# Layer 0's scale columns formed by TensorE products, its start-up sums spread over the steps, and the value projection 512 columns wide

## The chip, the cores and the metric

One core of one Trainium2 chip runs the whole program. The metric is device time in microseconds (us) of one execution, lower is better. TensorE's engine (PE) runs at one of two clock levels, 1.2 and 2.4 GHz; the profile gives the granted share of the higher one.

## The reference

Four layers over 1024 latent tokens of width 1024, with 256 context tokens beside them. Layer 0 is a pooling mixer, layer 1 a neighbourhood attention, layer 2 a short convolution, layer 3 pooling again. Each layer scales and shifts the normed input by columns that come from a conditioning vector. What the change touches is this, cut:

```python
def _modulation(cond, w, b):
    m = jax.nn.silu(cond) @ w + b
    return jnp.split(m, 3, axis=-1)          # shift, scale, gate

hx = _rmsnorm(x, norm_g[i]) * (1.0 + scale[:, None]) + shift[:, None]
hc = _rmsnorm(ctx, norm_g[i]) * (1.0 + cscale) + cshift   # from c_ctx
u, g = jnp.split(h @ w_in, 2, axis=-1)       # layer 0 (pool mixer)
q, k, v, g = jnp.split(h @ w_in, 4, axis=-1) # layer 1 (attention)
```

There are two conditioning vectors, `c` for the latent tokens (called x in the kernel) and `c_ctx` for the context (called c). For each layer, 1024 shift, 1024 scale and 1024 gate values are needed for x, and in layers 0 and 1 also for c.

## The kernel before

Features lie on the 128 partitions, so a 1024-wide activation is eight tiles, numbered k. Every fp32 matrix product is done in three passes (`mm3`, L115 to L117): operands are split into a high part (on ScalarE, `split`, L79) and a low part (L80, on VectorE or GpSimd), and high-high, high-low and low-high are added in PSUM.

The conditioning columns come 128 at a time. `ada_tile` (L166) takes a 128 by 1024 tile of the layer's modulation weights, loaded with a 512 KB transfer, multiplies it on VectorE with the broadcast silu row of one conditioning vector and sums along the row: one VectorE instruction and an accumulator read for one column of 128 values, so two for x and c.

`start` is the beginning of layer 0. Its order on VectorE, ScalarE, GpSimd and SP is the order of the code (`manual_schedule`); PE's is the order of the code everywhere. Its first part is the loop over k in which five output tiles (`FIRST`: u6, u7, g6, g7, g4) are multiplied over the first 512 latent tokens as the eight input tiles come in: for each k a weight tile is split, the scale column for x is summed (L166) and turned into a gain (`gain`, L174), then `high` (L698, ScalarE) and `low` (L702, VectorE) scale the input into its two parts, and 15 matmuls of 512 columns follow. Five of the sums for the context's scale ride in steps 2 to 6 (`EARLY`), the other three in the second part. The squares for the norm are formed on ScalarE and added on GpSimd (L734, L736). The second part multiplies the same five tiles over the other 512 tokens, and beside it come the eight shift tiles (`fetch_shift`, `ada`, `ada_sum`): for x always on VectorE; for c on VectorE for three of the eight (`DV`) and for the other five as a product on GpSimd (L793), a sum on ScalarE (L798) and an addition on GpSimd (L799). The third part multiplies the five tiles over the context (258 columns: 256 tokens and the two shift columns), which needs all the context's scale and shift columns (`gained_c`, L805/L806, and `shift_c`).

After `start` the remaining tiles of layer 0 follow, with the pooling sums (L455 to L466) and, as `background`, further conditioning tiles; the numbers in `RATES` say how many of these go with each weight load. There the tile scheduler sets the order on all engines but PE.

`na_first` is the beginning of layer 1. `v_block` forms the values for one block of 128 tokens and one range of output columns: here the activations are the stationary operand and the weights move. Before the change a block has 256 columns (a quarter of the width): 40 blocks of 24 matmuls, 40 evacuations to a tile `v` with three buffers (L970, L971) and 40 transfers out (L972). Between blocks hooks (`tick`) normalise the rest of layer 1's input, and `background(1)` runs one conditioning tile, from the sixth group of blocks on of layer 2.

PSUM has eight banks, taken in turn by everything that PE writes. The slots `a` (4 KB a partition) number 33. All transfers go through SP's queue, in order.

Of the kernel before, what the change touches and what calls it, by code (L numbers as in the profile page):

```python
# [24 lines left out]
P = 128  # L25
D = 1024
# [27 lines left out]
class Net:  # L54
# [102 lines left out]
    def ada_tile(self, l, conds, j, raw=None):  # L157
# [222 lines left out]
    def pool_in(self, li, h, chunks, start=None):  # L380
# [114 lines left out]
        RATES = (0,0,0,0,3,0,5,4,3,0,6,5,5,5,8,6) if 'c' in chunks else (3, 0, 6, 6) * 4  # L495
# [57 lines left out]
    def consts(self):  # L553
# [3 lines left out]
        rows = [self.slot([1, D]) for _ in range(2)]  # L557
# [3 lines left out]
        for f in range(2):  # L561
            nc.sync.dma_start(rows[f][:], i["conds"][f])
        nc.sync.dma_start(self.x0[0], i["xT"][0, :, 0:HALF])
# [3 lines left out]
        cond = [self.bank() for _ in range(4)]  # L567
        for f in range(4):
            nc.tensor.matmul(cond[f], self.ones[0:1, :], rows[f // 2][:, f % 2 * HALF:(f % 2 + 1) * HALF], start=True, stop=True)
        self.cond = cond[2:]  # L570
        self.sil["c"] = self.slot([P, D])
# [4 lines left out]
        self.shifts = self.pc.tile([P, 2, 3 * KT], F32, name="M0")  # L576
        for c in range(2):
            self.AB[0, "xc"[c]] = (self.pc.tile([P, KT], F32, name=f"A0{c}"), self.shifts[:, c, :])
# [71 lines left out]
    def start(self, h, put, shift, W):  # L650
# [7 lines left out]
        raws, shifts, wraw, parts = {}, {}, {}, {}  # L658
# [23 lines left out]

        fetch_w(0)
        nc.sync.dma_start(self.vec[:], i["vecs"])
        fetch(0)
        nc.sync.dma_start(x0[1], i["xT"][1, :, 0:HALF])
        fetch(1)
        fetch_w(1)
        self.load_pair(x0, i["xT"], 2, 0)
        fetch(2)  # L690
        fetch_w(2)
        row = self.sil["c"]
# [10 lines left out]

        def gain(k):
            self.ada_tile(0, ["x"], KT + k, raws[k])
            self.gain(0, "x", k, k + 1)

        split_weight(0)
        gain(0)
        high(0, x0, 0)  # L710
        low(0, x0, 0)
        for f in range(2):
            nc.scalar.activation(row[:, f * HALF:(f + 1) * HALF], self.cond[f], AF.Silu)
        gain(1)
        high(0, x0, 1)
        low(0, x0, 1)
        ps = {t: self.bank() for t in tiles}
# [20 lines left out]
        squares = {1: ((0, 0),), 2: ((0, 1),), 3: ((0, 2),), 4: ((0, 3),), 6: ((1, 0), (1, 1)), 7: ((1, 2), (1, 3))}  # L738
        EARLY = {2: (0,), 3: (1,), 4: (2,), 5: (3,), 6: (4,)}
        for k in range(KT):  # L740
            if k + 3 < KT:
                fetch(k + 3)
                if k + 3 < len(tiles):
                    fetch_w(k + 3)
                if k % 2:
                    self.load_pair(x0, i["xT"], k + 3, 0)
            if k == 4:
                nc.sync.dma_start(self.ident[:], i["ident"])
                for q in range(0, KT, 2):
                    self.load_pair(x1, i["xT"], q, HALF)  # L750
            if k == 5:
# [13 lines left out]
            if k >= 6:  # L765
                for q in range(4 * k - 24, 4 * k - 20):
                    high(1, x1, q)
                for q in range(4 * k - 24, 4):
                    low(1, x1, q)
            for ch, j in squares.get(k, ()):  # L770
                square(ch, (x0, x1)[ch], j)
            for n, t in enumerate(tiles):
                if (k, n) == (KT - 1, 2):
# [765 lines left out]
```

## Time and profile before

| what | value |
|---|---|
| median of 3 runs | 1920.62 us (1918.4 to 1920.69) |
| the profiled execution | 1921.01 us |
| its span, first to last instruction | 1919.2 us |
| PE busy | 1849.5 us, 96% of the span |
| VectorE (DVE) busy | 1090.0 us, 57% |
| ScalarE (ACT) busy | 725.2 us, 38% |
| GpSimd (POOL) busy | 568.6 us, 30% |
| mean granted PE clock | 0.986 |

Busy shares are means over stages that differ. The page's 40 slices (48 us each) show PE and DVE both at 7 to 9 tenths in the first six slices (0 to 288 us), and PE at 9 (90% or more) from then on but for the last slice. The times of single stages are read from the windows and rows below.

### The profile page before, as it was taken

The numbers are of one execution on the slowest core, as the hardware profiler recorded it, in microseconds if no ns is written. First come the engines' busy times: TensorE is split into PE (matmuls) and PEld (weight loads), VectorE is DVE, ScalarE is ACT, GpSimd is POOL, SyncE is SP. The second block draws the span as 40 slices with busy tenths as digits, with TensorE's granted clock in tenths as the row PEclk, the third lists the DMA queues.
The fourth block names the chain that finished last, engine by engine and source line by source line (L and its number), as shares of the span: only waits on it lengthen the run. The fifth ranks groups of instructions, "written<-read, shape, count | busy, mean of one in ns | idle before, by whom it ended". The sixth has DMA issues, their size and how long they took to land.

```text
span 1919.2 us, 27001 instructions
## 1 busy us (share of the span) xinstructions
PE 1849.5 (96%) x9808; PEld 1591.8 (83%) x9808; DVE 1090.0 (57%) x2251; ACT 725.2 (38%) x1401; POOL 568.6 (30%) x548
## 2 busy tenths in 40 slices
PE   7889899999999999999999999999999999999997
PEld 4677778889998889999998977888888887888887
DVE  7989977347441146766768678444232336433627
ACT  3332215344222146666657666121121225322422
POOL 4645412652210024444334542000000024433120
PEclk9899999999999999999999999999999999999999
DMA  6233352544673557676678656443111254011234
GB/s 256 77 105 105 114 175 79 184 139 145 224 251 116 165 154 210 196 205 189 192 210 231 201 176 202 132 132 99 44 45 55 70 183 159 12 49 41 77 119 155
DMA packets 126384, 272.10 MB, mean 142 GB/s; under 512 B 12810, under 2 KB 48394, under 8 KB 126252
## 3 DMA queue, kind: packets, MB, share of 16 engines
q1 hardware_dynamic: 126252, 270.39, 44.8%
q8 instruction: 77, 1.26, 0.3%
q14 instruction: 55, 0.45, 0.1%
HBM read 217.58 MB, written 52.76 MB: 141 GB/s over the span
## 4 chain that ended last, share of the span: by engine, by line
PE 76%; DVE 14%; issue 3%; DMA 3%; POOL 2%; ACT 1%; SPq 0%; DVEq 0%; POOLq 0%; ACTq 0%
PE mm L115 22%; PE mm L117 22%; PE mm L116 22%; DVE junk L166 4%; PE O L1257 4%; DMA raw<-in_ada 2%; PE T L1229 2%; PE TB L1229 2%; PE S L1172 1%; DVE S L455 1%; POOL S L455 1%; PE S L1173 1%; DVE a L80 1%; DVE wlo L80 1%; PE SC L1175 1%
## 5 line engine op out<-in xcount | busy, mean ns | idle before, releaser
L115 PE MATMUL mm<-a,whi 128*128 128x512 f32 (+2 forms) x2160 | 820.4, 380 | 23.7 <-DVE U L418 11.2
L116 PE MATMUL mm<-a,whi 128*128 128x512 f32 (+2 forms) x2149 | 804.5, 374 | 10.1 <-DVE a L80 8.0
L117 PE MATMUL mm<-a,wlo 128*128 128x512 f32 (+2 forms) x2160 | 806.6, 373 | 2.7 <-POOL wlo L80 2.6
L115 PEld LDWEIGHTS mm<-a,whi 128*128 128x128 f32 x2160 | 411.3, 190 | 96.7 <-DVE U L418 12.3
L116 PEld LDWEIGHTS mm<-a,whi 128*128 128x128 f32 x2149 | 409.6, 191 | 79.8 <-DVE a L80 9.4
L117 PEld LDWEIGHTS mm<-a,wlo 128*128 128x128 f32 x2160 | 410.7, 190 | 75.2 <-POOL wlo L80 4.1
L79 ACT ACTIVATE whi<-raw 128x1024 fp32r<-128x1024 f32 (+2 forms) x237 | 170.9, 739 | 352.3 <-PE mm L116 271.1
L80 POOL TENSOR_TENSOR wlo<-raw,whi 128x256 fp32r<-128x256 f32 (+2 forms) x150 | 191.3, 1289 | 365.8 <-ACT whi L79 338.7
L80 DVE TENSOR_TENSOR wlo<-raw,whi 128x1024 fp32r<-128x1024 f32 (+1 forms) x87 | 108.7, 1250 | 114.5 <-ACT whi L79 112.9
L166 DVE CUSTOM_DVE_ANT_0 junk<-raw,sil_x,vec 128x1024 bf16<-128x1024 f32 x86 | 118.6, 1379 | 92.9 <-DMA raw<-in_ada 92.3
L1208 POOL TENSOR_SCALAR lg<-lg,rsum 128x640 f32<-128x640 f32 (+1 forms) x128 | 99.2, 775 | 236.9 <-DVE rsum L1207 198.5
L115 PE MATMUL mm<-a,a 128*128 128x512 f32 (+2 forms) x280 | 98.1, 350 | 9.0 <-ACT a L698 7.1
L1199 ACT ACTIVATE lg<-lg,nmx 128x640 f32<-128x640 f32 (+1 forms) x128 | 102.6, 801 | 7.5 <-DVE rsum L1207 5.4
L224 POOL TENSOR_TENSOR a<-a,a 128x512 f32<-128x512 f32 x42 | 58.1, 1384 | 146.1 <-ACT a L223 139.9
L1187 DVE TENSOR_SCALAR_CACHE_REDUCE lg<-SC 128x256 f32<-128x256 f32 x128 | 54.2, 423 | 81.7 <-PE SC L1175 74.2
L116 PE MATMUL mm<-a,a 128*128 128x512 f32 (+2 forms) x275 | 96.2, 350 | 3.3 <-DVE a L702 2.8
L117 PE MATMUL mm<-a,a 128*128 128x512 f32 (+2 forms) x280 | 96.9, 346 | 0.5 <-DVE a L80 0.5
L1232 ACT ACTIVATE pthi<-TB 128x256 fp32r<-128x256 f32 (+1 forms) x128 | 52.6, 411 | 90.9 <-PE TB L1229 88.3
L1189 DVE CUSTOM_DVE_ANT_0 lg<-S,bias,mx 128x384 f32<-128x384 f32 (+1 forms) x128 | 74.8, 584 | 4.6
L1257 PE MATMUL O<-pthi,a 128*128 128x256 f32 (+2 forms) x288 | 76.6, 291 | 0.0
L1257 PE MATMUL O<-ptlo,a 128*128 128x256 f32 (+2 forms) x288 | 76.2, 293 | 0.0
L79 ACT ACTIVATE a<-a 128x512 fp32r<-128x512 f32 (+2 forms) x90 | 43.3, 536 | 79.3 <-POOL a L1420 72.7
(178 smaller groups left out, 2537.9 us busy)
## 6 DMA issues: line engine op xcount, KB each, us to landing
raw<-in_ada SPq DMA_DIRECT2D x86, 512.0 KB
raw<-in_pool_out SPq DMA_DIRECT2D x32, 512.0 KB
raw<-in_conv_in SPq DMA_DIRECT2D x32, 512.0 KB
raw<-in_pool_in SPq DMA_DIRECT2D x27, 512.0 KB
x<-a SPq DMA_DIRECT2D x48, 256.0 KB
raw<-in_na_in SPq DMA_DIRECT2D x24, 512.0 KB
a<-dk SPq DMA_DIRECT2D x48, 256.0 KB
dv<-v SPq DMA_DIRECT2D x40, 256.0 KB
```

Of the source, the lines that this page charges most:

```text
L79: self.nc.scalar.activation(hi, src, AF.Copy)
L80: (lo_engine or self.nc.vector).tensor_tensor(lo, src, hi.bitcast(F32), op=ALU.subtract)
L115: t.matmul(ps, wh, hh, start=(begin and k == ks[0]), stop=False)
L116: t.matmul(ps, wh, hl, start=False, stop=False)
L117: t.matmul(ps, wl, hh, start=False, stop=(end and k == ks[-1]))
L166: nc.vector.tensor_tensor_reduce(out=junk[:], in0=raw[:], in1=self.sil[c][:], scale=1.0, scalar=self.vec[:, b:b + 1], op0=ALU.mult, op1=AL ...
L224: (engine or nc.gpsimd).tensor_tensor(acc, acc, sq[k % 2], op=ALU.add)
L1189: nc.vector.tensor_tensor_reduce(out=lg[:, 0:L], in0=S[:, 0:L], in1=bias[:, off:off + L], scale=-1.0, scalar=mc[:], op0=ALU.add, op1=ALU.m ...
L1199: nc.scalar.activation(pr[:, :L + CTX], lg[:, :L + CTX], AF.Exp, bias=nm[:], scale=-1.0, accum_out=sm[:])
L1208: nc.gpsimd.tensor_scalar(pr[:, :L], pr[:, :L], rs[:], 1.0, op0=ALU.mult, op1=ALU.mult)
L1229: nc.tensor.transpose(t[:, s * P:(s + 1) * P], pr[:, o:o + P], self.ident[:])
L1257: nc.tensor.matmul(ops[:, q * P:(q + m) * P], v, part[:, p:p + m, :], start=not second and n == 0 and part is hi, stop=bool(second) and n ...
```

## The change

Three things are changed.

First, the scale columns of layer 0. A new input `ada0` holds the scale part of the layer's modulation weights laid out as matmul weights, and `condT` the two conditioning vectors as columns. `ada_product` multiplies one 128 by 1024 tile of it with the silu of both vectors: eight fp32 matmuls with two moving columns, which gives one 128-wide column for x and one for c at once in PSUM. `gain` then makes both gains in one DVE instruction from PSUM. The eight L166 sums for x and eight for c are gone, and the silu row for c now comes as a broadcast transfer and one activation in place of two matmuls.

Second, the order of `start`. The shift tiles 0 to 4 are summed for x and c on DVE in steps 0 to 4 of the first loop (`total`, `SUMS = 5`), tiles 5 to 7 in the second part; the detour over GpSimd and ScalarE is gone. The gain and high part of step k+2 are issued after the second tile of step k, its low part after the x sum. The high and low parts of the other 512 tokens are spread over steps 5 to 7, three at a time, and no longer fill the norm's chain. The weight tile u4 is loaded and split inside `start`, so two numbers of `RATES` change places.

Third, the value projection: blocks of 512 columns, so 20 blocks of 24 matmuls, 20 evacuations, 40 transfers out as before; eight weight tiles as before, five of them in `a` slots in place of three. `tick` runs twice in a block, `background` two or three times.

```diff
+    def ada_product(self, raw):
+        ps = self.bank()[:, 0:2]
+        for q in range(KT):
+            self.nc.tensor.matmul(ps, raw[:, q * P:(q + 1) * P], self.cols[:, 2 * q:2 * q + 2], start=q == 0, stop=q == KT - 1)
+        return ps
...
-        RATES = (0,0,0,0,3,0,5,4,3,0,6,5,5,5,8,6) if 'c' in chunks else (3, 0, 6, 6) * 4
+        RATES = (0,0,0,0,0,3,5,4,3,0,6,5,5,5,8,6) if 'c' in chunks else (3, 0, 6, 6) * 4
...
+        nc.sync.dma_start(rows[:], i["conds"][0])
+        nc.sync.dma_start(self.cols[:], i["condT"])
+        nc.scalar.activation(self.cols[:], self.cols[:], AF.Silu)
...
-            nc.sync.dma_start(raws[k][:], i["ada"][0, KT + k])
+            nc.sync.dma_start(raws[k][:], i["ada0"][k])
...
         def gain(k):
-            self.ada_tile(0, ["x"], KT + k, raws[k])
-            self.gain(0, "x", k, k + 1)
+            ps = self.ada_product(raws.pop(k))
+            nc.vector.tensor_scalar(self.gains[:, :, k], ps, up[:, k:k + 1], self.vec[:, V_NG + k:V_NG + k + 1],
+                                    op0=ALU.add, op1=ALU.mult)
+        def total(j, conds):
+            for c in conds:
+                self.ada_tile(0, [c], j, sums[j])
...
-            for q in EARLY.get(k, ()):
-                self.ada_tile(0, ["c"], KT + q, raws.pop(q))
+            if k >= SUMS:
+                for q in range(3 * (k - SUMS), min(3 * (k - SUMS) + 3, KT)):
+                    high(1, x1, q)
+                    low(1, x1, q)
+            for n, t in enumerate(tiles):
+                if n == 2 and k + 2 < KT:
+                    gain(k + 2)
+                    high(0, x0, k + 2)
+                if (k, n) == (KT - 1, 2):
+                    first = self.rstd_sums(([sq[0][:, 0]], HALF))
+                self.mm3(ps[t], self.wk(W[t]), lambda q: h[0][q], (k,), begin=k == 0, end=k == KT - 1)
+            if k < SUMS:
+                total(k, "x")
             if k + 2 < KT:
-                gain(k + 2)
-                high(0, x0, k + 2)
                 low(0, x0, k + 2)
+            if k < SUMS:
+                total(k, "c")
...
-            if k not in DV:
-                nc.gpsimd.tensor_tensor(raw[:], raw[:], row[:], op=ALU.mult)
...
-                nc.scalar.activation(raw[:], raw[:], AF.Copy, accum_out=Mc[:, k:k + 1])
...
             if n == 0:
-                step(0)
+                total(5, "xc")
+                W["u", 4] = self.weight(i["pool_in"][0, 4], own=True, lo_engine=nc.gpsimd)
+            if n == 1:
                 spread(0, dg)
...
-            ps = self.bank()[:, :256]
-            self.mm3(ps, hs, lambda k: tuple(Wv[k // 4][s][:, (k % 4) * 256:(k % 4 + 1) * 256] for s in range(2)), range(KT))
+            ps = self.bank()
+            for ks in (range(4), range(4, KT)):
+                self.mm3(ps[:], hs, lambda k: tuple(Wv[k // 2][s][:, k % 2 * HALF:(k % 2 + 1) * HALF] for s in range(2)), ks,
+                         begin=ks[0] == 0, end=ks[0] > 0)
+                self.tick()
...
-        blocks = [(0, (0, 1, 2, 3)), (1, (0, 1, 2, 3)), (0, (4, 5, 6, 7)), (1, (4, 5, 6, 7)), (0, (8, 9)), (1, (8, 9)),
-                  (2, range(NB + 2)), (3, range(NB + 2))]
+        blocks = [(0, (0, 1, 2, 3)), (0, (4, 5, 6, 7)), (0, (8, 9)), (1, range(NB + 2))]
...
-                self.background(1)
+                self.background(3 if n == 3 else 2)
```

How the change moves instructions is shown at three places.

On DVE before, from one step of the first loop to the next: `junk` rows are L166 sums (with `sil_x` for x, with `a_154`, the silu row of c, for c), `A_159` is the gain column and the L702 row is the low part.

```order
L166 ISA junk_284,M_158<-a_244,sil_x,vec 128x1024
L166 ISA M_158 128x1
L174 SCALAR_TENSOR_TENSOR A_159<-M_158,vec 128x1
L702 SCALAR_TENSOR_TENSOR a_287<-a_134,A_159,a_287 128x512
L166 ISA junk_315,M_158<-a_178,a_154,vec 128x1024
```

On DVE in the changed kernel, the same stretch: the gain (L724) reads `mm_333`, a product in PSUM, and the low part is L716.

```order
L724 TENSOR_SCALAR A_154<-mm_333,up_186,vec 128x2
L166 ISA junk_354,M_153<-a_276,sil_x,vec 128x1024
L166 ISA M_153 128x1
L716 SCALAR_TENSOR_TENSOR a_343<-a_134,A_154,a_343 128x512
L166 ISA junk_357,M_153<-a_276,a_180,vec 128x1024
```

The sum no longer stands ahead of the gain that comes from it; a sum of a shift tile stands between the gain and the low part, where ScalarE forms the high part.

On PE in the changed kernel, between the second and the third tile of a step (before, the fifteen matmuls of a step stood without a break): `mm_381` is the product of the scale tile of the step after next.

```order
L117 MATMUL mm_220<-a_298,wlo_279 128x512
L174 MATMUL mm_381<-cols,a_272 128x2 x8
L115 MATMUL mm_221<-a_298,whi_278 128x512
L116 MATMUL mm_221<-a_298,whi_278 128x512
L117 MATMUL mm_221<-a_298,wlo_279 128x512
```

Eight small products are put into each of steps 0 to 5, and sixteen stand ahead of the first step.

On PE in a value block before: the tile `a_3229` of the activations is loaded as the weights and 256 columns of `whi_3707` and `wlo_3708` move.

```order
L115 MATMUL mm_3729<-whi_3707,a_3229 128x256
L116 MATMUL mm_3729<-wlo_3708,a_3229 128x256
L117 MATMUL mm_3729<-whi_3707,a_3229 128x256
L115 MATMUL mm_3729<-whi_3707,a_3230 128x256
L116 MATMUL mm_3729<-wlo_3708,a_3230 128x256
```

On PE in a value block of the changed kernel:

```order
L115 MATMUL mm_3761<-whi_3745,a_3261 128x512
L116 MATMUL mm_3761<-wlo_3746,a_3261 128x512
L117 MATMUL mm_3761<-whi_3745,a_3261 128x512
L115 MATMUL mm_3761<-whi_3745,a_3262 128x512
L116 MATMUL mm_3761<-wlo_3746,a_3262 128x512
```

The rows are the same but for their width, and there are 480 of them in place of 960.

## Rows read from the trace of the kernel before

**Rows 1.** Windows: length, busy (count) of PE, PEld, DVE, ACT, POOL; clock, DMA, GB/s

```profile
20.00:30.00 10.00, 9.04 (x39) 6.73 (x37) 9.08 (x8) 3.59 (x5) 5.61 (x2) 1.00 1.04 393
...
100.00:125.00 25.00, 17.43 (x123) 16.55 (x122) 21.41 (x43) 6.96 (x17) 8.18 (x16) 0.86 0.28 89
...
175.00:200.00 25.00, 24.31 (x125) 20.70 (x124) 24.03 (x36) 3.83 (x7) 15.30 (x12) 1.00 0.29 94
...
500.00:525.00 25.00, 25.00 (x211) 25.00 (x210) 14.12 (x25) 3.63 (x9) 4.66 (x2) 1.00 0.79 269
...
600.00:625.00 25.00, 25.00 (x112) 20.71 (x111) 2.70 (x3) 4.29 (x6) 0.00 (x0) 1.00 0.36 123
```

**Rows 2.** Timeline, one step of the first loop: start us, us, engine, line

```profile
32.47 3.22 POOL L734 TENSOR_TENSOR a<-a,a 128x1024 f32<-128x1024 f32 x1 [3.06 <-ACT a L730]
33.46 3.30 DVE L166 CUSTOM_DVE_ANT_0 junk<-a,sil_x,vec 128x1024 bf16<-128x1024 f32 x1
35.64 3.32 POOL L80 TENSOR_TENSOR a<-a,a 128x1024 fp32r<-128x1024 f32 x1
36.81 2.17 DVE L174 SCALAR_TENSOR_TENSOR A<-M,vec 128x1 f32<-128x1 f32 x1
39.01 0.72 ACT L698 ACTIVATE a<-a,A 128x512 fp32r<-128x512 f32 x1 [5.67 <-DVE A L174]
39.77 0.75 DVE L702 SCALAR_TENSOR_TENSOR a<-a,A,a 128x512 fp32r<-128x512 f32 x1 [0.79 <-ACT a L698]
39.79 0.80 PE L115 MATMUL mm<-a,a 128*128 128x512 f32 x1 [4.03 <-ACT a L698]
40.44 1.28 DVE L166 CUSTOM_DVE_ANT_0 junk<-a,a,vec 128x1024 bf16<-128x1024 f32 x1
```

**Rows 3.** PE's waits in 0-40, 40-75, 75-120 us: us, times, longest

```profile
PE mm L115 <- ACT a L698: 8.9, 3, 4.0
...
PE mm L115 <- ACT a L698: 7.1, 3, 4.0
...
PE mm L116 <- DVE a L80: 7.6, 3, 5.2
```

**Rows 4.** Timeline of PE: matmuls at either clock level, and fp32 products

```profile
2.30 7.16 PE L569 MATMUL mm<-a,ones 1*128 1x512 f32 x8 [2.30 <-DMA a<-in_conds]
...
34.24 0.39 PE L115 MATMUL mm<-a,whi 128*128 128x512 f32 x1
34.46 0.39 PE L116 MATMUL mm<-a,whi 128*128 128x512 f32 x1
...
41.17 0.63 PE L117 MATMUL mm<-a,a 128*128 128x512 f32 x1
41.59 0.63 PE L115 MATMUL mm<-a,a 128*128 128x512 f32 x1
...
55.74 1.70 PE L240 MATMUL mm<-ones,a 128*128 128x1 f32 x8
...
77.28 1.02 PE L240 MATMUL mm<-ones,a 128*128 128x1 f32 x8 [0.48 <-ACT a L723]
```

**Rows 5.** Timeline of PE: where the three parts of start begin and end

```profile
12.13 0.79 PE L115 MATMUL mm<-a,whi 128*128 128x512 f32 x1 [2.67 <-ACT a L698]
...
61.29 0.58 PE L115 MATMUL mm<-a,whi 128*128 128x512 f32 x1
...
125.66 0.28 PE L117 MATMUL mm<-a,a 128*128 128x258 f32 x1
```

**Rows 6.** Groups by line, 0 to 126 us: busy us, mean ns, idle before

```profile
L793 POOL TENSOR_TENSOR raw<-raw,a 128x1024 f32<-128x1024 f32 x3 | 7.3, 2448 | 5.0 <-DVE nv L251 3.8 <-DVE a L80 1.2
```

**Rows 7.** Timeline of ScalarE: evacuations of two value blocks in turn

```profile
490.59 0.39 ACT L970 ACTIVATE v<-mm 128x256 fp32r<-128x256 f32 x1 [2.50 <-PE mm L117]
493.47 0.38 ACT L970 ACTIVATE v<-mm 128x256 fp32r<-128x256 f32 x1 [2.50 <-PE mm L117]
```

**Rows 8.** The chain that ended last: a transfer of 512 KB, start us and us

```profile
111.78 3.63 DMA raw<-in_ada
```

More of the change, by code (lines that the diff above doesn't have):

```diff
@@ L556, in consts @@
         self.x0 = self.xtiles()
-        rows = [self.slot([1, D]) for _ in range(2)]
+        rows = self.slot([1, D])
         self.vec = self.pc.tile([P, V_ALL], F32, name="vec")
@@ L560, in consts @@
         self.edge = self.pc.tile([P, 64], F32, name="edge")
-        for f in range(2):
-            nc.sync.dma_start(rows[f][:], i["conds"][f])
-        nc.sync.dma_start(self.x0[0], i["xT"][0, :, 0:HALF])
+        self.cols = self.pc.tile([P, 2 * KT], F32, name="cols")
+        nc.sync.dma_start(rows[:], i["conds"][0])
+        nc.sync.dma_start(self.cols[:], i["condT"])
+        nc.scalar.activation(self.cols[:], self.cols[:], AF.Silu)
         self.ones = self.pc.tile([P, P], F32, name="ones")
         nc.vector.memset(self.ones[:], 1.0)
[L567 to L571, printed above, removed]
+        cond = [self.bank() for _ in range(2)]
+        for f in range(2):
+            nc.tensor.matmul(cond[f], self.ones[0:1, :], rows[:, f * HALF:(f + 1) * HALF], start=True, stop=True)
         self.sil["x"] = self.pc.tile([P, D], F32, name="sil_x")
@@ L657, in start @@
         x0 = self.x0
-        raws, shifts, wraw, parts = {}, {}, {}, {}
+        raws, sums, wraw, parts = {}, {}, {}, {}
         A, M = self.AB[0, "x"]
@@ L702, in low @@
             nc.vector.scalar_tensor_tensor(lo, x[k], A[:, k:k + 1], hi.bitcast(F32), op0=ALU.mult, op1=ALU.subtract)
+        up = self.small([P, KT], tag="up", bufs=1)
+        nc.vector.tensor_scalar(up[:], self.vec[:, V_AB + KT:V_AB + 2 * KT], 1.0, None, op0=ALU.add)
         def gain(k):
-            self.ada_tile(0, ["x"], KT + k, raws[k])
-            self.gain(0, "x", k, k + 1)
-        split_weight(0)
+            ps = self.ada_product(raws.pop(k))
[4 more added lines that the diff above has]
+                self.ada_tile(0, [c], j, sums[j])
+            if "c" in conds:
+                del sums[j]
         gain(0)
         high(0, x0, 0)
+        split_weight(0)
         low(0, x0, 0)
-        for f in range(2):
-            nc.scalar.activation(row[:, f * HALF:(f + 1) * HALF], self.cond[f], AF.Silu)
         gain(1)
@@ L761, in start @@
+            if k < SUMS:
+                total(k, "x")
             if k + 2 < KT:
-                gain(k + 2)
-                high(0, x0, k + 2)
                 low(0, x0, k + 2)
[L765 to L769, printed above, removed]
+            if k < SUMS:
+                total(k, "c")
             for ch, j in squares.get(k, ()):
                 square(ch, (x0, x1)[ch], j)
-            for n, t in enumerate(tiles):
-                if (k, n) == (KT - 1, 2):
-                    sums = self.rstd_sums(([sq[0][:, 0]], HALF))
-                self.mm3(ps[t], self.wk(W[t]), lambda q: h[0][q], (k,), begin=k == 0, end=k == KT - 1)
@@ L776, in start @@
-        dg = self.rstd_chain(sums, [lambda q=q: low(1, x1, q) for q in range(4, KT)])
+        dg = self.rstd_chain(first)
         ps0 = ps
         Ac, Mc = self.AB[0, "c"]
-        def fetch_shift(k):
-            if k < 2:
-                shifts[k] = self.slot([P, D])[:]
-            elif k == 4:
-                shifts[k] = self.pt.tile([P, 16 + SEQ + 16], F32, tag="U", name=self.nm("raw"), bufs=3)[:, 0:D]
-            else:
-                shifts[k] = self.pw.tile([P, D], F32, tag="raw", name=self.nm("raw"), bufs=3)[:]
-            nc.sync.dma_start(shifts[k], i["ada"][0, k])
@@ L812, in start @@
         nc.sync.dma_start(self.edge[:], i["edge"])
-        for k in range(KT):
-            fetch_shift(k)
+        for k in range(SUMS, KT):
+            fetch_sum(k)
         stc = self.sumsq_start(CTX)
         waiting = []
-        def step(k):
-            ada(k)
-            if k:
-                ada_sum(k - 1)
         for n, t in enumerate(tiles):
```

103 lines of the change are left out of this document (44 added, 59 removed).

## The prediction

> **What bounds the kernel now.** I read the windows first, to see where PE is not full. From 300 us on it is: the stretches at 500 and 600 us show 25.00 of 25 us busy at a granted clock of 1.00 [rows 1]. Work taken off PE there shortens the run one for one; work taken off another engine there is worth nothing. Before 300 us it is otherwise. In 100 to 125 us PE has 17.43 us of 25 and a clock of 0.86, while DVE has 21.41; in 175 to 200 us DVE has 24.03 [rows 1]. So the beginning is DVE's, and what sets DVE's pace is to be found there.
>
> The timeline of one step shows it [rows 2]. A POOL instruction starts at 32.47 and another stands behind it at 35.64. Each takes 3.2 to 3.3 us, where a like one takes 2.4 when it is let through [rows 6]. The DVE sum that starts at 33.46 takes 3.30 us where the next takes 1.28 at 40.44; the gain, one element per partition, takes 2.17. The two engines take turns: while one holds, the other's started instruction stands. So for DVE's instructions of this kind the times of DVE and POOL add. Behind the sum and the gain come the high part (ACT, 0.72), and only then PE's first matmul of the step, which waited 4.03 us [rows 2]. PE's waits for that high part sum to 8.9 us by 40 us and to 7.1 by 75; later it waits 7.6 us for the low parts of the context's shift columns (L80), 5.2 of them at once [rows 3].
>
> The sum is made against the profiled execution, 1921.0 us (span 1919.2); the median is 0.4 below it, so what I take off goes off either.
>
> **Value projection.** One block before takes 490.59 to 493.47, 2.88 us for 24 matmuls of 256 columns [rows 7]; 40 blocks make 115.2. By the count in 500 to 525 us, 25 / 211 = 0.1185 each, 960 make 113.7. A 512-column matmul follows the last by 0.22 to 0.23: 34.24 to 34.46 [rows 4], and 25 / 112 = 0.223 by 600 to 625 us [rows 1]; 480 make 107.1, with 0.226 they make 108.5. The gain lies between 113.7 - 108.5 = 5 and 115.2 - 107.1 = 8; I take 7, since the evacuation rows have no gap of their own in them. PE is full here, so this goes through to the end, if transfers follow. They have to: thirty calls of the background now fall on ten blocks in place of twenty. Eight of those blocks each ask for three loads and the values out, 4 times 0.52 MB, 2.1 MB in 5.4 us, 390 GB/s. In 20 to 30 us plain loads moved 393; in 500 to 525 us, with values going out, 269 at a DMA share of 0.79, some 340 if full [rows 1]. At 340 a block takes 6.2 us and eight blocks fall 6 us behind. PE has eight banks and `v` three buffers ahead of it, some 40 us of cover; without it the loss would be those 6 us. Weight loads, their splits and the transfers out are as many as before and hidden by the same full PE: nothing.
>
> **Start, removed from DVE and POOL.** Sums on DVE fall from 8 + 8 (scale) + 8 + 3 (shift) = 27 to 16: 11 fewer at 1.28 us [rows 2], 14.1 us. The five POOL products, 2.4 us each [rows 6], 12 us, go too, and as POOL's time adds to DVE's here they can be worth as much again. The five sums and additions on ACT and POOL were waited for by the context's last columns only. So the beginning can gain up to 26 us.
>
> **Start, added to PE.** A product is eight fp32 matmuls, in the trace two passes each: the eight passes of 1.02 us at the high level and 1.70 at the low one [rows 4] make 2.0 and 3.4 us per product. Sixteen passes, twice, stand ahead of the first matmul, at the low level: 6.8 us. The two matmuls for c's row go away (half of 7.16, 3.6 us [rows 4]). PE's queue: rows of the condition from 2.3 to 5.9, products to 12.7, against 12.13 for the first matmul before [rows 5]: 0.6 us late, nothing gained. The six others, 12 us, stand among the matmuls. A step is then 15 x 0.226 + 2.0 = 5.4 us on PE.
>
> **Start, first part.** DVE per step: two sums 2.56, a low part 0.75 [rows 2], a gain of at most 0.2 (what is left of its 2.17 when POOL's instruction ends at 38.96), 3.5 us. POOL's splits and squares (five at 2.4, three at 2.4, one shorter) are 21 us over eight steps, 2.6 per step. They add to 6.1, above PE's 5.4; DVE still sets the pace. From the third gain at some 18.5 us (6 matmuls at 0.42 and a product behind 12.7) five steps take 30.5 us, to 49. Three low parts of the other half and the last gain follow, 52; its high part, and the last step of 3.4 us, 57. Before, the second part began at 61.3 [rows 5]. What PE waits for is then DVE's sum of work, no longer the chain sum, gain, high part within one step, since a gain is two steps ahead.
>
> A rule speaks against part of this. The rows show a gain of one element held for 2.17 us by POOL [rows 2]. The Trainium skill (SBUF — State Buffer, Who interferes with whom) says that a DVE instruction with two SBUF inputs contends with a GpSimd instruction that reads SBUF, and one with at most one such input does not. The new gain reads PSUM and so would go free; the sums and low parts, with two, would not. If the new gain were held as the old one is, 2 us in half of eight steps, the sum for the start would be 8 us smaller.
>
> **Start, second and third part.** After the first part DVE has the rest of the low parts, the norm's chain, three tiles of sums (8 us in place of 14 sums and POOL's five products) and the context's 16 small low parts. By the same adding I put the norm's columns at 66 (before 69.7), the five tiles of the second half at 5.4 us each, with one stop for the norm, to 91, and the last of the context's rows at 92 to 95. The third part is 120 matmuls of 0.12 us and a pause for the norm, 15 us: it ends at 107 to 110, where before it ended at 125.7 after 7.6 us of waits [rows 3, 5]. That is 16 to 19 us; I take **17**. The count says 14 to 26. The low bound is 4, what the first part alone gives (61.3 - 57); the high one 26.
>
> **After start.** DVE stays full (24.03 of 25 us in 175 to 200 [rows 1]), with the same work in nearly the same order: two numbers in `RATES` change places, and one split (POOL 2.4 us) is done earlier. So the lead should be carried, not eaten; the weights for u4 no longer wait for buffers that the shift tiles held. I give this 0, between -3 (the split out of the way) and +3 (two more `a` slots held).
>
> **Sum.** 1921.0 - 7 - 17 = 1897.0; off the median 1896.6. I take **1897**.
>
> **Rivals.** *The lead is small.* SP's queue is in order, and the sums' tiles now stand in it among the scale tiles. A 512 KB load takes 3.63 us from issue to use when alone [rows 8]; if DVE stops at four of the sums for that, 14 us of the 17 go, and what is left is 3 + 7: 1911. For it: DVE's order is fixed, and a late tile holds the gain behind it. Against: the loop's 11.5 MB at the 393 GB/s of 20 to 30 us [rows 1] are in by 32 us, before DVE reaches the fourth sum.
>
> *The value blocks do not gain.* The transfers bound that stage and PE waits: 1921 - 17 = 1904. Against it the banks above.
>
> *Slower: the clock stays low.* The fp32 products keep PE lightly used, and the granted clock, 0.86 in 100 to 125 us [rows 1], could lie at the low level through all of `start`. Matmuls then follow at 0.42 us (41.17 to 41.59 [rows 4]) and products cost 3.4: first part 6 x 9.7 + 2 x 6.3 = 71 from 12.7, to 84; second part 51 and 3, to 138; third 26, to 164. That is 38 later than 125.7; less 7 it gives 1952. It turns the result once a good two fifths of it happen (8 us lost in place of 17 won, the 7 gone), that is when the mean granted clock of 13 to 110 us falls below some 0.75. Against it: from 34 to 77 us the trace has the high level, the low one and the high one again [rows 4], and 175 to 200 us is at 1.00 [rows 1].
> The Trainium skill (TensorE: Matmul & The Clock Gate, Part 1) has it that the throttled state is the default and activity releases it; the rows at 41 and 34 us agree on two levels. By that rule the clock stays low for as long as such products fail to release it, which gives the time above; no row here shows whether they do.
>
> **How the numbers follow.** Forecast 0.65 (its own range 1888 to 1904); small lead 0.18; no gain in the value blocks 0.08; low clock 0.05; the rest, such as a lead above 26 us, 0.04. The range reaches from 1921 - 26 - 8 = 1887 to the small lead, 1911. A measurement can tell 0.2%, 3.8 us, from no change. Faster by more needs only one of the two gains: the first three cases and half of the rest, 0.93. Slower is the low clock but for its mildest fifth, 0.04; within 0.2% lies that fifth and the other half of the rest, 0.03.
>
> **What would show it.** Right: the first part of `start` ends at 55 to 59 us, the last matmul of 258 columns at 107 to 110, the new gain takes 0.2 to 0.3 us beside POOL, value blocks follow at 5.4 us with PE full. Wrong: PE's waits for a high part still sum to over 10 us, DVE waits for the shift tiles' loads, a granted clock under 0.8 in 25 to 100 us, PE idle between 500 and 560 us, or an end of `start` that is early while 300 us comes at the same place as before.

## The result, and the profile after

The changed kernel takes 1894.41 us (median of 4 runs, 1893.05 to 1895.18), the kernel before 1920.06 beside it: 25.7 us less, ratio 0.9867 with a 95% interval of 0.985 to 0.9884. The profiled execution has a span of 1893.4 us (before 1919.2) and a mean granted clock of 0.991 (0.986).

First come the windows of the kernel after, with the columns of [rows 1]:

```profile
25.00:50.00 25.00, 25.00 (x149) 21.93 (x149) 21.70 (x25) 10.45 (x13) 15.81 (x6) 1.00 0.79 290
...
100.00:125.00 25.00, 25.00 (x159) 22.72 (x159) 21.42 (x33) 11.84 (x21) 15.35 (x15) 1.00 0.39 127
...
175.00:200.00 25.00, 21.65 (x110) 17.81 (x108) 22.74 (x37) 4.03 (x8) 7.59 (x8) 1.00 0.45 137
...
500.00:525.00 25.00, 25.00 (x112) 20.69 (x111) 16.98 (x27) 3.00 (x5) 0.00 (x0) 1.00 0.94 317
```

In 100 to 125 us PE is full, where it had 17.43 of 25 us before (start is over at 106 us now); in 500 to 525 it is as full as before, with 112 matmuls of 512 columns in place of 211 of 256; in 175 to 200 DVE is still the fuller of the two.

Where start's parts begin and end shows in PE's timeline (start us, us): the first matmul, the first one of the second part, the last of start. They answer to [rows 5].

```profile
13.46 0.77 PE L115 MATMUL mm<-a,whi 128*128 128x512 f32 x1
...
59.01 0.39 PE L115 MATMUL mm<-a,whi 128*128 128x512 f32 x1
...
106.07 0.28 PE L117 MATMUL mm<-a,a 128*128 128x258 f32 x1
```

Start ends at 106.07, 19.6 us ahead of before; 17.3 of that come in the second and third part (47.1 us for 64.4), 2.3 in the first. PE's waits (us in all, times, longest) from 59 to 106 us, which answer to the last row of [rows 3], are nearly gone:

```profile
PE mm L115 <- ACT a L747: 0.7, 1, 0.7
PE mm L285 <- DVE a L278: 0.2, 1, 0.2
```

Later marks are the lines that evacuate PSUM (a ScalarE or VectorE line's first and last start): the residuals of the pooling output (`xo`) and, behind the values, the keys. The first two rows are of after, the other two of before.

```profile
L369 DVE SCALAR_TENSOR_TENSOR a<-mm,M,xo x24: 471/750/756, 319.1 to 422.6; 128x512 f32<-128x512 f32 x16, 128x256 f32<-128x256 f32 x8
...
L875 ACT ACTIVATE a<-mm x24: 368/592/600, 539.7 to 989.0; 128x512 fp32r<-128x512 f32 x16, 128x256 fp32r<-128x256 f32 x8
```

```profile
L362 DVE SCALAR_TENSOR_TENSOR a<-mm,M,xo x24: 472/750/751, 341.3 to 445.6; 128x512 f32<-128x512 f32 x16, 128x256 f32<-128x256 f32 x8
...
L889 ACT ACTIVATE a<-mm x24: 365/592/602, 568.1 to 1016.6; 128x512 fp32r<-128x512 f32 x16, 128x256 fp32r<-128x256 f32 x8
```

So the lead is 22.2 us at 319, 23.0 at 422, and 28.4 at 540, behind the values. At the end of the span it is 25.8. The values themselves are best read on PE, from their first matmul to their last (timeline of PE, the first two rows of after, the other two of before):

```profile
422.35 0.40 PE L115 MATMUL mm<-whi,a 128*128 128x512 f32 x1
...
533.79 0.39 PE L117 MATMUL mm<-a,a 128*128 128x512 f32 x1
```

```profile
444.55 0.28 PE L115 MATMUL mm<-whi,a 128*128 128x256 f32 x1
...
562.27 0.28 PE L117 MATMUL mm<-whi,a 128*128 128x256 f32 x1
```

By these the lead is 22.2 us where the values begin and 28.5 where they end.

### The profile page after: what moved, and what is told of

Same layout as the page of the kernel before. It is cut to its first block, busy times and chain, and to the rows that moved or that the text cites. A ratio compares the mean times of both kernels' runs of the same rounds, so it can differ in the third digit from the quotient of the medians.

```text
span 1893.4 us, 26177 instructions
## 1 busy us (share of the span) xinstructions
PE 1847.6 (98%) x9452; PEld 1579.8 (83%) x9452; DVE 1058.8 (56%) x2209; ACT 717.3 (38%) x1371; POOL 548.5 (29%) x538
## 4 chain that ended last, share of the span: by engine, by line
PE 79%; DVE 11%; DMA 4%; issue 3%; POOL 2%; ACT 1%; SPq 0%; DVEq 0%; POOLq 0%; ACTq 0%
PE mm L115 23%; PE mm L117 22%; PE mm L116 22%; PE O L1245 4%; DVE junk L166 3%; DMA raw<-in_ada 2%; PE T L1217 2%; PE TB L1217 2%; PE S L1160 1%; DVE a L80 1%; DMA a<-in_ada 1%; PE S L1161 1%; DVE S L462 1%; PE SC L1163 1%; PE SC L1162 1%
## 5 line engine op out<-in xcount | busy, mean ns | idle before, releaser
L115 PE MATMUL mm<-a,whi 128*128 128x512 f32 (+2 forms) x2136 | 810.7, 380 | 15.9 <-DVE U L425 8.2
L117 PE MATMUL mm<-a,wlo 128*128 128x512 f32 (+2 forms) x2136 | 797.1, 373 | 2.1 <-POOL wlo L80 2.0
L116 PE MATMUL mm<-a,whi 128*128 128x512 f32 (+2 forms) x2126 | 794.1, 374 | 2.2 <-DVE a L318 1.3
L115 PEld LDWEIGHTS mm<-a,whi 128*128 128x128 f32 x2136 | 405.8, 190 | 85.1 <-DVE U L425 9.8
L117 PEld LDWEIGHTS mm<-a,wlo 128*128 128x128 f32 x2136 | 405.4, 190 | 75.1 <-POOL wlo L80 3.5
L116 PEld LDWEIGHTS mm<-a,whi 128*128 128x128 f32 x2126 | 404.0, 190 | 69.1 <-DVE a L318 2.2
L80 POOL TENSOR_TENSOR wlo<-raw,whi 128x256 fp32r<-128x256 f32 (+2 forms) x147 | 181.7, 1250 | 388.6 <-ACT whi L79 364.4
L166 DVE CUSTOM_DVE_ANT_0 junk<-raw,sil_x,vec 128x1024 bf16<-128x1024 f32 x80 | 113.3, 1416 | 80.1 <-DMA raw<-in_ada 79.5
L115 PE MATMUL mm<-a,a 128*128 128x512 f32 (+1 forms) x284 | 109.9, 387 | 2.2 <-ACT a L79 1.1
L117 PE MATMUL mm<-a,a 128*128 128x512 f32 (+1 forms) x284 | 108.8, 383 | 0.5 <-DVE a L80 0.5
L116 PE MATMUL mm<-a,a 128*128 128x512 f32 (+1 forms) x278 | 107.0, 385 | 0.3 <-DVE a L716 0.3
```

What stands on the lines that cost most here:

```text
L80: (lo_engine or self.nc.vector).tensor_tensor(lo, src, hi.bitcast(F32), op=ALU.subtract)
L115: t.matmul(ps, wh, hh, start=(begin and k == ks[0]), stop=False)
L116: t.matmul(ps, wh, hl, start=False, stop=False)
L117: t.matmul(ps, wl, hh, start=False, stop=(end and k == ks[-1]))
L166: nc.vector.tensor_tensor_reduce(out=junk[:], in0=raw[:], in1=self.sil[c][:], scale=1.0, scalar=self.vec[:, b:b + 1], op0=ALU.mult, op1=AL ...
```

## Experiments: the two halves apart

**Only the values.** The kernel before with the value projection of after.

```
-  ps = self.bank()[:, :256]      # 40 blocks of 24 matmuls
+  ps = self.bank()               # 20 blocks, 512 columns
```

> The kernel before, with the value projection of the kernel after and nothing else of the change. In the trace after, the blocks' evacuations follow at 5.44 us (before 2.88 for half the columns), and the offset between the two kernels grows by 5.4 us over that stage (from -23.0 at the last evacuation of the layer-0 output projection to -28.4 at the first key evacuation). If the two halves of the change add, and this stage keeps what it gains: 1920.1 - 5.4 = 1914.7 us. Rival: the 2.6 us by which the offset shrinks later, through the attention (-28.4 at its first logits, -25.8 at the end), belong to the new value layout; then 1917.3. If the gain of this stage hangs on the earlier start of it (the transfers out stand otherwise against other loads), 1920 and no offset after the stage.

Measured: 1915.75 us, 4.6 less than the 1920.32 beside it, ratio 0.9975 (0.9964 to 0.9986). The interval is 1913.4 to 1917.6 us and holds both the first number and the rival's 1917.3, so the time alone does not decide between them; the trace does. It has a lead of 5.5 us at the first key (562.6 for 568.1) and keeps 5.2 to the last residual of layer 3 (1901.8 for 1907.0): the new layout gives nothing back, and the rival falls. On PE its values begin 0.7 us late (445.24) and end 5.6 early (556.71), so that the stage itself wins 6.3, as in after.

**Only the start.** The kernel after with the values of before.

> The kernel after with the value projection of the kernel before (40 blocks of 256 columns, one step of the background each): the change to the start alone. In the trace after, start ends at 106.1 (before 125.7), and the offset is -23.0 at 422 us. If that is kept: 1920.1 - 23.0 = 1897.1; with the shrinking of the attention (2.6) in it, 1899.7. Prediction's number for this part alone was -17, 1903. Rival: the value blocks give the 2.6 back and not the start, then 1897. Start's end at 106.1 in any case.

Measured: 1899.03, 21.3 less, ratio 0.989 (0.9874 to 0.9906). Start ends at 107.7, not at 106.1 as expected (the last section has why). 21.3 and 4.6 add to 25.9, against 25.7 for both: within the intervals the halves add.

## Experiments: what sets the pace of the first part

The trace after seemed to contradict the prediction: PE full from 25 to 50 us, and DVE waiting for the products. This is the greatest of DVE's waits in 0 to 60 us (us in all, times, longest):

```profile
DVE A L724 <- PE mm L174: 15.1, 5, 4.2
```

**Half of each product left out.** Four of a product's eight matmuls are not done, so half of the sum is missing.

```
-  for q in range(KT):
+  for q in range(0, KT, 2):
       self.nc.tensor.matmul(ps, raw[...], self.cols[...], ...)
```

> The kernel after with every second of the eight matmuls of a scale product left out (half of the sum over the inputs is missing from the scale columns): 64 passes less of PE, nothing changed on DVE. Theory A, read from the trace after: PE sets the pace of the first part of start (DVE waits 15.1 us for the products). Then 6 products lose 0.85 us each at the high level and 2 lose 1.7 at the low one: the second part begins 8.5 us earlier, at 50.5 in place of 59.0, as far as DVE's slack reaches, and the run takes 1886 to 1889. Theory B, as the prediction had it: DVE and POOL set the pace at 6.1 us per step. Then at most the two products ahead of the first matmul count, 3.4 us at its start and less at the end: second part at 56 to 59, run 1892 to 1894.

Measured: 1893.85, which cannot be told from after. The first matmul came 2.0 us earlier, the second part 0.5. What PE won it lost in one wait, and its matmuls then followed 0.43 us apart, the low level (timeline of PE):

```profile
42.26 0.79 PE L116 MATMUL mm<-a,a 128*128 128x512 f32 x1 [4.16 <-DVE a L716]
42.85 0.63 PE L117 MATMUL mm<-a,a 128*128 128x512 f32 x1
43.27 0.63 PE L115 MATMUL mm<-a,a 128*128 128x512 f32 x1
```

So theory B holds. In the kernel after, the five waits of DVE are over at 31.65 us; from there to the end of the first part it stops for nothing but 0.85 us, and the last gain hangs on it.

The run of the start alone shows the same with nothing left out. Its first part is the code of after, but PE's matmuls came to the high level there at 16.1 us in place of 22.6 (the last section). Compare the 34 us that end with the last of the eight gains, first in that run and then in after (columns of [rows 1]):

```profile
18.00:52.00 34.00, 32.09 (x179) 27.13 (x178) 33.82 (x34) 12.43 (x15) 22.47 (x8) 1.00 0.79 294
```

```profile
19.00:53.00 34.00, 33.95 (x182) 29.03 (x182) 28.34 (x34) 12.23 (x15) 20.27 (x8) 1.00 0.78 292
```

With PE ahead, DVE is full: from its third gain to its last it takes 33.8 us and stops for 0.2 of them. In after it takes 33.2 us and stops for 5.0, the last two of its five waits. What DVE no longer waits for PE it is held beside POOL instead: over this stretch its sums and low parts take 9.4 us more than their 1.28 and 0.75 each in after, 15.1 in the start alone and 15.4 with half products. That is why lighter products hardly move the last gain (51.72 us with half of them, 52.85 in after). These rows (timeline, DVE and POOL) answer to [rows 2]:

```profile
36.05 3.40 POOL L80 TENSOR_TENSOR a<-a,a 128x1024 fp32r<-128x1024 f32 x1
37.11 0.08 DVE L166 DVE_READ_ACCUMULATOR2_ANT M<- 128x1 f32 x1
37.11 0.27 DVE L724 TENSOR_SCALAR A<-mm,up,vec 128x2 f32<-128x2 f32 x1
37.30 3.23 DVE L166 CUSTOM_DVE_ANT_0 junk<-a,sil_x,vec 128x1024 bf16<-128x1024 f32 x1
...
39.41 3.34 POOL L758 TENSOR_TENSOR a<-a,a 128x1024 f32<-128x1024 f32 x1
...
40.46 2.84 DVE L716 SCALAR_TENSOR_TENSOR a<-a,A,a 128x512 fp32r<-128x512 f32 x1
```

```profile
47.69 5.24 DVE L716 SCALAR_TENSOR_TENSOR a<-a,A,a 128x512 fp32r<-128x512 f32 x3
52.85 0.27 DVE L724 TENSOR_SCALAR A<-mm,up,vec 128x2 f32<-128x2 f32 x1
```

Sums and low parts still take turns with POOL (3.23 for 1.28, 2.84 for 0.75); the gain does not.

**The five tiles' sums back in the second part.**

```
-  if k < SUMS: total(k, "x") ... total(k, "c")       # in the steps
+  for j in (0, 1, 5): total(j, "xc")                 # behind group 0
+  for j in (2, 3, 6): total(j, "xc")                 # behind group 1
+  for j in (4, 7): total(j, "xc")                    # behind group 2
```

> The kernel after with the sums of shift tiles 0 to 4 (ten DVE instructions of 1.28 us, longer where POOL holds) taken out of the first part's steps and done in the second part, three tiles behind the first group of matmuls, three behind the second, two behind the third. Theory A (PE sets the first part's pace): the first part keeps its end at 59.0 within 0.5 us; DVE's 13 us and more are added to a second part in which DVE is busy 31.6 of 32.4 us, so the context's rows come 10 to 14 us later, PE waits for them, start ends at 114 to 120, and the run takes 1903 to 1908. Theory B (DVE sets the first part's pace): the first part ends 8 to 13 us earlier, the second as much later, start ends within 3 us of 106.1, and the run is within 3 us of 1894.4.

Measured: 1901.49, 7.1 above after; ratio to before 0.9914 (0.9884 to 0.9943). Neither theory had all of it. The first part ended at 54.8, 4.2 earlier (B), but there PE was full and DVE waited 2 to 3 us for each product, so PE was the pace then. Two things make the 4.2. PE's matmuls had come to the high level at 16.7 us, in after at 22.6; by the spacings of 0.43 and 0.23 us these 5.9 us are worth some 2.7 (an estimate). The rest is what PE waits in the first part of after, 1.3 us (timeline of PE):

```profile
53.99 0.49 PE L115 MATMUL mm<-a,a 128*128 128x512 f32 x1 [1.03 <-ACT a L712]
54.77 0.50 PE L116 MATMUL mm<-a,a 128*128 128x512 f32 x1 [0.29 <-DVE a L716]
```

Where the matmuls rose as early with the sums in place, in the run of the start alone, the first part ended at 61.1, so that the sums are worth 6 us there. The second and third part gave back 12.3, with PE waiting 8.2 for a norm's columns (row below, waits of 55 to 115 us), and start ended at 114.1.

```profile
PE mm L285 <- DVE a L278: 8.2, 1, 8.2
```

Read together: with DVE lightened by 13 us of sums the first part wins 1 to 6, as PE's clock rises late or early, and stops at PE's pace; with PE lightened it wins 0.5 and stops at DVE's. DVE is last, PE close behind, and of the two places tried the sums cost less where the change put them.

**The scale columns as DVE sums again.**

```
-  ps = self.ada_product(raws.pop(k)); nc.vector.tensor_scalar(self.gains[:, :, k], ps, ...)
+  self.ada_tile(0, ["x"], KT + k, raws[k]); self.gain(0, "x", k, k + 1)
+  self.ada_tile(0, ["c"], KT + k, raws.pop(k))       # at the end of the step
```

> The kernel after with the scale columns as sums on DVE again (16 instructions of 1.28 us, the sum of x at the place of the product, that of c at the end of the same step), all else of the change kept. By the reading that DVE and POOL together set the pace of the first part (run with half of the products: products half as long, first part 0.5 us shorter), 8 products leave PE and some 20 us of sums come to DVE, 15 of them in the six steps, and more where POOL holds them: first part ends at 72 to 80 in place of 59, start at 120 to 128, run 1908 to 1918. Rival: PE sets the pace and is 13 us lighter without the products: first part ends before 59 and the run takes under 1894.

Measured: 1910.58, 16.2 above after (14.8 by the two ratios to the kernel before); ratio to before 0.9944 (0.9929 to 0.9959). First part to 73, start to 121.2, as expected. The products are the greater part of the gain, at least in this order, where the shift tiles' sums stand in the same steps. What the rest of the start wins without them is 10.5 less the values' 4.6, some 6 us. The window of this kernel's first part, with the columns of [rows 1], is DVE's:

```profile
31.00:73.00 42.00, 28.55 (x79) 20.67 (x78) 40.86 (x48) 15.37 (x20) 19.41 (x8) 0.71 0.35 124
```

**Five of c's sums on POOL and ACT again.**

```
-  if k < SUMS: total(k, "c")
+  if 0 < k <= SUMS: nc.scalar.activation(raw[:], raw[:], AF.Copy, accum_out=col); nc.gpsimd.tensor_tensor(col, ...)
+  if k < SUMS: nc.gpsimd.tensor_tensor(sums[k][:], sums[k][:], row[:], op=ALU.mult)
```

> The kernel after with c's sums of shift tiles 0 to 4 taken from DVE (5 of 1.28 us, 6.4 us) and done by POOL and ACT as before the change (a product on POOL, 2.4 us each when let through, 12 us, a sum on ACT, a one-column addition on POOL). If the times of DVE and POOL add in this stretch, the first part becomes 12 - 6.4 = 5.6 us longer (and the five additions): it ends at 63 to 66, run 1897 to 1901. If the two engines work side by side, DVE is 6.4 us lighter and the first part ends as early as PE allows, at 55 to 58, run 1889 to 1894.

Measured: 1900.98, 6.6 above after (5.0 by the ratios), within the first range; but the trace shows another cause. DVE was idle between its instructions until 43 us. Then a sum on ACT waited for POOL's product, and behind it in ACT's queue stood the high parts (timeline of ACT):

```profile
48.09 1.06 ACT L802 ACTIVATE a<-a 128x1024 f32<-128x1024 f32 x1 [4.37 <-POOL a L805]
49.06 0.18 ACT L802 ACTIVATION_READ_ACCUMULATOR a<-a 128x1 f32 x1
49.15 1.04 ACT L754 ACTIVATE a<-a 128x1024 f32<-128x1024 f32 x1
50.09 1.93 ACT L712 ACTIVATE a<-a,A 128x512 fp32r<-128x512 f32 x3
```

DVE stood 4.99 us for these, the last gain came at 57.80, and PE waited 5.45. So the run says that the detour costs 5 to 7 us here, not that the times of DVE and POOL add; for that the rows and windows above stand.

## Experiments: behind start

**The early weight of u4 undone.**

```
-  W["u", 4] = self.weight(i["pool_in"][0, 4], own=True, lo_engine=nc.gpsimd)
-  RATES = (0,0,0,0,0,3,5,4, ...
+  RATES = (0,0,0,0,3,0,5,4, ...
```

> The kernel after with the weight of u4 loaded and split where it was before, behind start, and the two numbers of the table that changed places set back: the one thing of the change that acts on the stretch between start's end and 320 us. In the traces that stretch takes 215.5 us before (125.8 to 341.3) and 212.9 after (106.2 to 319.1). Theory A: the early weight makes those 2.6 us; then start ends near 106 as before the edit, 319.1 becomes 321 to 322, and the run takes 1896 to 1897.5. Theory B: they are a matter of what DVE had left over from start, and the edit does nothing: 1894 to 1895.

Measured: 1894.32, as after; from start's end to 319.6 it takes 213.8 us (after 213.1, before 215.7). Theory A falls: of its 2.6 us 0.8 are there at most. PE's waits on this stretch are 17.7 us before, 14.7 after and 16.8 in this run, so the early weight may spare PE some waiting, which one profile does not show; what makes the stretch shorter than before stays open.

**Other rates, and eight sums elsewhere.** DVE does 52 background sums in 106 to 262 us, and PE waits there. Four runs tried to use that. The first changed the table of rates; the second took the eight sums of layer 1's gate to the value blocks, the third did that and evened the rates; the fourth had the eight begin at the fifth value block.

> The kernel after with other numbers in the table of background steps (2, 3, 3, 0, 3, 3, 4, 5, 3, 0 in place of 3, 4, 3, 0, 6, 5, 5, 5, 8, 6 for the ten tiles that load a weight; five steps of 35 left for the output projection). In the trace after DVE is 20 to 24 of 25 us busy from 106 to 250, 52 background sums among it, and PE waits 14.9 us there, 4.3 at 202.8 behind six steps at one tile; from 320 to 345 DVE is busy 3.75 of 25. If those waits are the sums' doing, 4 to 10 us of them go: 1884 to 1890. If they are the shift sums' and splits' own, 1893 to 1895; if the sums left over hold the first norm of the output projection, later than 1895.

> The kernel after with the eight background sums of the third part of layer 1 (one per tile, 1.28 us each, 10 us of DVE) taken out of the pool stage and done in the first ten value blocks, where DVE is busy 12 of 15 us or less and nothing waits for it; the table of rates as it is. In the trace after these eight stand last among the 52, at 246 to 262 us, ahead of PE waits of 4.2 us at 256 to 268. If DVE is the cause of those waits, 3 to 5 us go: 1889.5 to 1891.5. If PE's waits there come from the window sums of the mix and not from the background, 1893.5 to 1895.5. If the value stage has no room for them, later than that stage's 5.44 us per block and above 1895.

> As the run before it, with the remaining 27 steps more evenly over the tiles (3, 4, 3, 1, 4, 4, 4, 4, 1, 0 in place of 3, 4, 3, 0, 6, 5, 5, 5, 8, 6). The run with other rates got slower by 5.5 us, with one wait of 9.9 us behind nine steps that came to two tiles in a row while DVE was late. If the number of steps per tile decides, the wait of 4.3 us at 202.8 goes as well and the run takes 1885 to 1889; if the sum of DVE's work up to a tile decides, only the waits change places and it takes 1889 to 1895.

> As the run with the eight sums in the first ten value blocks, but from the fifth block on. There the pool stage ended 7.2 us earlier (first evacuation of the output projection at 311.9, after 319.1), and 3.1 us were lost at 427.6, where PE waited for the columns of a norm whose chain on DVE had two sums among it. If those sums are the cause, the wait goes and the run takes 1886 to 1889; if the wait comes whatever stands there, 1890 to 1892.

Measured: 1899.96, 1890.96, 1896.12 and 1892.18. Both evened tables made it worse (the second against the run with the gate's sums moved alone), by a new wait at 253 and at 246.5 us, of 9.9 and 5.1 (timeline of PE in the first of them):

```profile
253.06 0.80 PE L115 MATMUL mm<-a,whi 128*128 128x512 f32 x1 [9.94 <-DVE Uc L420]
```

With the gate's sums moved the first residual came at 311.9 (after 319.1), but PE lost 3.1 to a norm at 427.6. In the last run it lost 3.4 there as well, for the scheduler, which sets DVE's order in that stage, had put the sums among the norm's chain again although the code stands behind it (timeline of DVE):

```profile
426.45 0.16 DVE L268 SCALAR_TENSOR_TENSOR nu<-nu,nv 128x4 f32<-128x4 f32 x1
426.53 1.28 DVE L166 CUSTOM_DVE_ANT_0 junk<-raw,sil_x,vec 128x1024 bf16<-128x1024 f32 x1
...
427.73 0.15 DVE L272 SCALAR_TENSOR_TENSOR ny<-nu,ny 128x4 f32<-128x4 f32 x1
```

So that run did not test its theory. The intervals of these two (0.9827 to 0.9853 and 0.9837 to 0.9878) touch or overlap that of after; a version better than after is not shown.

**After once more, beside the last of them.**

> The kernel after, unchanged, on the same chip as the run ahead of it, so that the two can be compared, and as a second profile: 1893 to 1896. The end of start lay between 105.9 and 108.2 us in four profiles whose code is the same up to there; if that scatter comes from when the matmul spacing falls from 0.43 to 0.23 us (16 to 23 us in them), an early fall goes with an early end; if DVE sets the pace, the two are unrelated.

Measured: 1893.28. Its profile keeps what the first gave back: from the first key evacuation to the last residual of layer 3 it takes 1338.9 us, as before (1338.9), where the first profile of after took 1341.5. Over all profiles of the study this stretch takes 1338.7 to 1343.0. So the 2.6 us lost behind 540 us are scatter of single executions and not the change; a sum of leads from two traces is good to 2 or 3 us.

## Why the prediction was right

1897 was forecast, 2.6 above the 1894.4 measured. The sum was -17 - 7 + 0 for start, values and the stretch behind start; in the traces it is -19.6, -6.3 and -2.6 (-28.5, of which the profiled execution lost 2.6 again to scatter), and -21.3 and -4.6 in the runs of the halves. The mechanism is borne out: DVE's sums set the pace of the first part, and the values win by their width. That the total comes so close is in part luck: within start the first part won 2.0 us less than put and the rest 4.6 more, and the 2.6 won behind start, put at nothing, stand against as much lost to scatter.

**First part: right, with PE closer than put.** The last gain was forecast at 52 and came at 52.85; the second part at 57 and came at 59.01, at the late edge of the 55 to 59 that were named as its sign. 0.8 of that is the first matmul, at 13.46 for 12.7; the last step is the other part: from 52 to 57 was allowed, and it took 52.85 to 59.01, for the eight matmuls of the norm's sums in it (0.95 us) were left out, and its first matmul waited for high and low part. "DVE still sets the pace" is borne out by the run with half products and by the start alone. An even pace of 6.1 us per step is not what after shows: its gains follow at 5.25 and 5.46 us from 26.40 to 37.11, PE's pace, and at 7.32 and 8.42 behind, DVE's. The sum put 13 us of POOL's time on DVE's five steps and no wait for PE; the trace of after has 9.4 us of the one and 5.0 of the other, so that the 52 is right there partly by chance. In the start alone it is right as meant: 33.5 us were put from the third gain to the last, and there they are 33.8, without waits. PE's products were sized right (2.0 forecast, 1.84 at the high level; 3.4 and 3.57 at the low one).

**Second and third part: the term that was mis-sized.** Forecast were the norm's columns at 66, the context's last rows at 92 to 95 and the end at 107 to 110. The columns came at 70.6, held by POOL's squares and by its low part of u4 (the rows below), which cost PE 1 us and no more; the last low part was done by 89, ahead of PE's 91.38, so that no wait was left; 106.07 is 2.6 us better than the sum of 17 has it, and before the 107 to 110 that were named as the sign. From the second part's start to start's end 12.7 us were to be won, and 17.3 were. The first two rows are of after, a step of the norm's chain (0.16 us when let through) and the columns' last instructions; the third is of before, where POOL let these through (timelines of DVE):

```profile
59.14 2.27 DVE L267 TENSOR_TENSOR nu<-ny 128x4 f32<-128x4 f32 x1
...
66.67 4.03 DVE L278 TENSOR_SCALAR a<-ident,ny 128x128 f32<-128x128 f32 x4
```

```profile
69.82 0.87 DVE L271 TENSOR_SCALAR a<-ident,ny 128x128 f32<-128x128 f32 x4
```

Adding all of POOL's time to DVE's was too much all the same, since DVE's instructions that read PSUM are not held (timeline, two evacuations of 0.64 us each beside POOL's squares; such a square beside a sum, the last row, takes 1.66 us, where the three of the first row take 2.64):

```profile
72.82 2.64 POOL L231 TENSOR_TENSOR a<-a 128x256 f32<-128x256 f32 x3 [2.45 <-ACT a L230]
...
73.15 1.28 DVE L425 TENSOR_TENSOR U<-mm,a 128x512 f32<-128x512 f32 x2
...
76.36 1.66 POOL L231 TENSOR_TENSOR a<-a 128x256 f32<-128x256 f32 x1
```

**After start: 0 forecast, -2.6 measured** (316.3 us from start's end to the first matmul of the values at 422.35, before 318.9 to 444.55), within the -3 allowed. The residual rows would have it at -3.4; 0.9 of that is the place of the last residual beside the first value matmul, 1.07 us behind it before and 0.20 in after and in the values alone.

**Values: -7 forecast, -6.3 in the trace, -4.6 alone** (2.7 to 6.9 by its interval). Blocks follow at 5.44 us, as said (timeline of ACT):

```profile
496.14 0.60 ACT L959 ACTIVATE v<-mm 128x512 fp32r<-128x512 f32 x1 [4.84 <-PE mm L117]
501.58 0.60 ACT L959 ACTIVATE v<-mm 128x512 fp32r<-128x512 f32 x1 [4.84 <-DMA dv<-v]
```

Twenty of 5.44 are 108.8, forty of 2.88 [rows 7] 115.2: 6.4, the middle of the bounds, and from first matmul to last it is 111.4 us for 117.7. The 7 was 0.7 too much. Transfers moved 317 GB/s at a share of 0.94, and PE waited for none.

**The rivals.** Late loads: DVE waited for no sum's tile in the profile of after. Low clock: the granted clock is 1.00 in 25 to 125 us. The gain held by POOL: the row at 37.11 us shows 0.27 beside a POOL instruction from 36.05 to 39.45, where the old gain took 2.17 [rows 2]. The rule of the Trainium skill (SBUF — State Buffer, Who interferes with whom) agrees with that, and with the sum at 37.30 that reads two rows from SBUF and was held. The Trainium skill states there the free case only outside DVE's two-port modes, which the prediction left out. It matters, for an instruction with a single tile from SBUF was held here as well: L278 at 66.67 us, 4.03 us for four beside POOL, where the like four took 0.87 before. In which mode it ran no row shows.

## What to carry to other kernels

Where two engines take turns, moving work to a third pays even if the third then looks full: PE took 19.8 us of products, 128 passes, was busy for all of 25 to 50 us, and the run got some 15 us shorter. Work that a later stage waits for belongs beside the earlier stage, as far as that engine's pace allows; of the two tables that spread the sums behind start more evenly, both made the run longer. Before a trace's full engine is called the bound, make its work shorter: half of the products gone changed nothing. And where two engines take turns, the waits of one are no slack: DVE reached its instructions sooner and was held by POOL for as long.

## What the runs showed that was not expected

PE's matmuls begin at a spacing of 0.43 us in every profile, the low level, and the spacing falls to 0.23 at a time that differs between executions. The column of the granted clock does not show this: it reads 1.00 for 13.4 to 22.6 us in after, because the trace's record of the clock begins only at the rise (22.8 us), so ahead of it the spacing has to be read. With the same code in the first part, the fall came at 16.1, 16.3 and 16.5 us in three profiles and at 22.6 to 25.1 in five; and start ended at 107.7 to 109.9 in the three, at 105.8 to 107.1 in the five. The early fall goes with the late end, which the expectation of the last run had the other way round or not at all. PE comes before DVE's last parts, waits 0.9 to 1.9 us twice, and its matmuls follow at the low level again (the start alone, timeline of PE and window of the stretch):

```profile
52.91 0.50 PE L115 MATMUL mm<-a,a 128*128 128x512 f32 x1 [1.74 <-ACT a L712]
53.70 0.80 PE L116 MATMUL mm<-a,a 128*128 128x512 f32 x1 [0.28 <-DVE a L716]
54.30 0.63 PE L117 MATMUL mm<-a,a 128*128 128x512 f32 x1
```

```profile
50.00:62.00 12.00, 9.97 (x33) 7.76 (x32) 10.27 (x14) 7.57 (x10) 4.03 (x2) 0.72 0.52 174
```

The last gain comes at 51.8 to 52.5 us in the three and at 52.9 to 53.9 in the five, but from it to the second part it is 9.3 to 9.8 us in the three and 6.2 in the five. So a faster start of PE is worth 1 us at the last gain, and the low level behind it costs 3: one more sign that DVE sets the pace.
